# Two attention heads at a time on the two halves of TensorE's array, and value products that come out transposed

## The chip, the cores and the metric

The kernel runs on one core of one Trainium2 chip. TensorE (PE) multiplies matrices into PSUM, VectorE (DVE) and ScalarE (ACT) work element by element, GpSimd (POOL) and SyncE (SP) do little here but set up and start transfers. The metric is the device time of one execution in microseconds, the median of several runs.

## The reference

Two layers over 256 tokens of width 1024 in float32. Each layer is x += 1/2 norm(FFN), x += norm(mixer), x += 1/2 norm(FFN). The mixer of the first layer is the dilated attention that the change is about; that of the second is a retention.

```python
def banded_attention(q, k, v, bias, radius):
    ...
    s = jnp.einsum('nbqhd,nbkhd->nbhqk', qb, kw).astype(jnp.float32) * (dh ** -0.5) + bias_blk
    s = jnp.where(valid[None, :, None], s, NEG_INF)
    smax = jnp.max(s, axis=-1, keepdims=True)
    p = jnp.exp(s - smax)
    denom = jnp.sum(p, axis=-1, keepdims=True)
    o = jnp.einsum('nbhqk,nbkhd->nbqhd', (p / denom).astype(v.dtype), vw)
    lse = (smax + jnp.log(denom))[..., 0]
    ...

def dilated_attention(h, w_in, w_out, rel_bias):
    proj = (h @ w_in).reshape(B, S, N_GROUPS, 3, H_A, DH_A)
    # three groups, (window, dilation) = (128, 1), (512, 4), (2048, 16): 16 heads of 64 each
    ...
    wts = jax.nn.softmax(jnp.stack(lses, axis=0), axis=0)
    o = jnp.einsum('gbsh,gbshd->bshd', wts.astype(h.dtype), jnp.stack(outs, axis=0))
    return o.reshape(B, S, D_A) @ w_out
```

Merging the three groups by their softmax denominators is the same as one softmax over the keys of all three groups. The kernel does that.

## The kernel before, in words

Everything is one sequence of weight products with small work in between. All weights stream from DRAM in their order of use (`Stream`): a transfer of 1 MB lands in `raw`, ScalarE writes its rounded part `whi`, VectorE the rest `wlo` (lines 109 to 116), and each product is three matmuls, x_hi·w_hi, x_hi·w_lo and x_lo·w_hi (`mm3`, lines 182 to 184). A piece is a quarter of a unit of 512 columns (1024 for the output weights), 12 matmuls of 128x512; a ring holds six pieces that are split ahead of their use.

`attn` goes through two octets of heads (o = 0, 1), each with nine units: q and k of the three groups, then v of the three. The tokens are in two tiles T of 128. After a unit its PSUM sums are evicted; q and k are transposed at line 624 (`qk_store`). Work between the pieces waits in two lists: `pend` is emptied after a unit's second piece, and after each piece two entries of `bg` are taken (`unit`, `work`). After the last k, `push` puts the softmax of 16 (token tile, head) combinations into `bg`, one step for each, with head i's scores in step i, its exponential in step i + 1 and its transposes in step i + 2; so two steps run after each piece of the v units:

- `sm_scores`: q of the head is 64 rows of `qk`, on partitions 0-63 or 64-127. One product with the 256 keys of group 0 (line 644) and four small ones, 64x64, for groups 1 and 2 (line 649, written to the rows of either half of the tokens); a custom VectorE instruction adds the bias and takes the minimum (line 652).
- `sm_exp`: ScalarE's exponential with the sum into `den` (line 659).
- `sm_trans`: three transposes into a bank `ptt` (line 665) and a copy into `PT`, by ScalarE for odd i (667), by VectorE for even i (669).

`pv` multiplies, for each of eight heads, `PT` as the stationary operand with 64 columns of `V` as the moving one (lines 680, 681, and 683 for either half of the rows), so the output `ob` has tokens in rows; VectorE divides by the denominators (685, 687). `o_store` transposes the result (line 696) and splits it into `ot` (699, 700). For the first octet `pv` and `o_store` are in `bg` and run within the next unit; for the second they are hooks between the rows of the output projection `down`.

PSUM has a pool of six banks for sums (`acc`: scores, products, value products) and one of two for transposes (`trb`). The instructions of an engine are ordered by a scheduler from the order in which the program issues them, except in the first unit and at the end of `down`, where the order is written out.

## Time and profile before

| | |
|---|---|
| median of 3 runs | 1352.9 us (1352.35 to 1353.52) |
| profiled execution, from first to last instruction | 1351.3 us |
| PE busy | 1335.3 us, 99% |
| VectorE busy | 855.0 us, 63% |
| ScalarE busy | 710.9 us, 53% |
| DMA | 235.46 MB, mean 174 GB/s |
| softmax of the two octets | about 285 to 330 and 428 to 474 us |
| value products | 339 to 353, 482 to 489, 492 to 498 us |

The profiled execution has no time of its own beside its span; the median of the runs is 1.6 us above the span. In the lines of the profile, `PE` is a matmul and `PEld` a weight load; `out<-in` are the program's tiles, followed by rows*columns of the stationary operand and rows x columns of the moving one; L644 is line 644 of the kernel. A product in plain float32 has two records. The records of matmuls overlap, since they are pipelined: what a matmul costs is read from the starts of its neighbours.

### The profile page before, as it was taken

Reading aid. Unit: us, or ns where it says so; the run is one execution under the profiler, and the core shown is the slowest. Engines: PE = TensorE matmul, PEld = TensorE weight load, DVE = VectorE, ACT = ScalarE, POOL = GpSimd, SP = SyncE. Lnnn points to the kernel's source line nnn. Section 1 sums busy time; section 2 is a strip of 40 time slices with the busy share of each in tenths; the row PEclk is TensorE's granted clock in tenths of the full one; section 3 lists DMA queues with packets and bytes.
Section 4 is the critical chain, followed back from the end, with each engine's and each line's share of the span. In section 5 each row is a group of like instructions: output and inputs, shape, how many; then the busy total and the mean of one; then the engine's idle time right before and its main releaser. Section 6 shows DMA issues by size and latency. Waiting matters only on the chain.

```text
span 1351.3 us, 16684 instructions
## 1 busy us (share of the span) xinstructions
PE 1335.3 (99%) x6342; PEld 1077.1 (80%) x6342; DVE 855.0 (63%) x1501; ACT 710.9 (53%) x1103; POOL 19.2 (1%) x16
## 2 busy tenths in 40 slices
PE   8999999999999999999999999999999999999997
PEld 6878887877887787888888888877888888888886
DVE  5756556575355547866557665479888775766544
ACT  4655455565355535865454655355555544565532
POOL 1000001000000001000000000000000000000000
PEclk8999999999999999999999999999999999999999
DMA  7755557753574235655555655556555545465551
GB/s 208 240 169 186 187 200 181 210 187 109 134 209 156 95 116 170 206 187 186 186 187 177 201 185 174 186 161 194 156 162 158 178 151 192 154 204 188 187 187 63
DMA packets 129693, 235.46 MB, mean 174 GB/s; under 512 B 25020, under 2 KB 41900, under 8 KB 129613
## 3 DMA queue, kind: packets, MB, share of 16 engines
q1 hardware_dynamic: 129468, 234.14, 54.6%
q8 instruction: 50, 0.82, 0.2%
q10 hardware_dynamic: 144, 0.26, 0.1%
q14 instruction: 31, 0.25, 0.1%
HBM read 232.21 MB, written 1.12 MB: 173 GB/s over the span
## 4 chain that ended last, share of the span: by engine, by line
PE 93%; DVE 3%; DMA 2%; ACT 1%; issue 1%; SPq 0%; DVEq 0%; ACTq 0%
PE ac_f L184 11%; PE ac_f L183 11%; PE ac_f L182 11%; PE d_f L182 6%; PE d_f L184 6%; PE d_f L183 6%; PE at L182 5%; PE at L184 5%; PE at L183 5%; PE rt L183 4%; PE rt L184 4%; PE rt L182 4%; PE sc L644 1%; PE htr L340 1%; PE d_rt L182 1%; PE d_rt L184 1%
## 5 line engine op out<-in xcount | busy, mean ns | idle before, releaser
L116 DVE SCALAR_TENSOR_TENSOR wlo<-raw,gcol,whi 128x512 fp32r<-128x512 f32 x596 | 418.3, 749 | 216.6 <-ACT whi L115 215.8
L115 ACT ACTIVATE whi<-raw,gcol 128x512 fp32r<-128x512 f32 x596 | 393.3, 715 | 295.6 <-PE ac_f L184 83.8
L110 DVE TENSOR_TENSOR wlo<-raw,whi 128x1024 fp32r<-128x1024 f32 x112 | 137.2, 1225 | 147.7 <-ACT whi L109 147.7
L109 ACT ACTIVATE whi<-raw 128x1024 fp32r<-128x1024 f32 x112 | 118.7, 1060 | 178.8 <-PE d_f L184 103.9
L182 PE MATMUL d_f<-whi,hhf 128*128 128x512 f32 x352 | 140.7, 400 | 0.0
L184 PE MATMUL d_f<-whi,hlf 128*128 128x512 f32 x352 | 138.7, 394 | 0.0
L183 PE MATMUL d_f<-wlo,hhf 128*128 128x512 f32 x352 | 138.2, 393 | 0.0
L182 PE MATMUL at<-whi,xh_f 128*128 128x512 f32 x276 | 111.4, 404 | 0.0
L184 PE MATMUL at<-whi,xl_f 128*128 128x512 f32 x276 | 108.4, 393 | 0.0
L183 PE MATMUL at<-wlo,xh_f 128*128 128x512 f32 x276 | 107.6, 390 | 0.0
L183 PE MATMUL rt<-wlo,xh_f 128*128 128x512 f32 x244 | 97.3, 399 | 0.0
L182 PE MATMUL rt<-whi,xh_f 128*128 128x512 f32 x244 | 96.7, 396 | 0.0
L184 PE MATMUL rt<-whi,xl_f 128*128 128x512 f32 x244 | 96.4, 395 | 0.0
L184 PEld LDWEIGHTS d_f<-whi,hlf 128*128 128x128 f32 x352 | 66.1, 188 | 16.9
L183 PEld LDWEIGHTS d_f<-wlo,hhf 128*128 128x128 f32 x352 | 66.1, 188 | 15.5
L182 PEld LDWEIGHTS d_f<-whi,hhf 128*128 128x128 f32 x352 | 66.1, 188 | 15.1
L182 PE MATMUL ac_f<-whi,xh_in 128*128 128x512 f32 x176 | 71.2, 405 | 2.9 <-ACT whi L115 2.7
L184 PE MATMUL ac_f<-whi,xl_in 128*128 128x512 f32 x176 | 69.9, 397 | 0.0
L183 PE MATMUL ac_f<-wlo,xh_in 128*128 128x512 f32 x176 | 69.7, 396 | 0.2 <-DVE wlo L116 0.2
L182 PE MATMUL ac_f<-whi,xh_at 128*128 128x512 f32 x168 | 66.6, 397 | 0.2 <-ACT xh_at L224 0.2
L184 PE MATMUL ac_f<-whi,xl_at 128*128 128x512 f32 x168 | 65.9, 392 | 0.0
L183 PE MATMUL ac_f<-wlo,xh_at 128*128 128x512 f32 x168 | 65.4, 389 | 0.0
(294 smaller groups left out, 2223.0 us busy)
## 6 DMA issues: line engine op xcount, KB each, us to landing
raw<-in_ffn_w_down_dram SPq DMA_DIRECT2D x44, 1024.0 KB, 4.9
raw<-in_ffn_w_up_dram SPq DMA_DIRECT2D x40, 1024.0 KB, 5.1
raw<-in_ffn_w_gate_dram SPq DMA_DIRECT2D x39, 1024.0 KB, 5.1
raw<-in_attn_w_in_dram SPq DMA_DIRECT2D x36, 1024.0 KB, 5.2
raw<-in_ret_w_in_dram SPq DMA_DIRECT2D x24, 1024.0 KB, 5.3
raw<-in_ret_w_in_dram SPq DMA_DIRECT2D x16, 512.0 KB, 4.0
raw<-in_ret_w_out_dram SPq DMA_DIRECT2D x8, 1024.0 KB, 5.0
raw<-in_ffn_w_gate_dram SPq DMA_DIRECT2D x10, 512.0 KB, 4.0
```

Source lines behind the costliest of these rows:

```text
L109: nc.scalar.activation(hi, raw, AF.Copy)
L110: nc.vector.tensor_tensor(out=lo, in0=raw, in1=hi.bitcast(F32), op=ALU.subtract)
L115: nc.scalar.activation(hi[:, s], raw[:, s], AF.Copy, scale=gc)
L116: nc.vector.scalar_tensor_tensor(out=lo[:, s], in0=raw[:, s], scalar=gc, in1=hi[:, s].bitcast(F32), op0=ALU.mult, op1=ALU.subtract,)
L182: mm(out, xh, wh, start=start, stop=False)
L183: mm(out, xh, wl, start=False, stop=False)
L184: mm(out, xl, wh, start=False, stop=stop)
L340: nc.tensor.transpose(tr[:, k * P : (k + 1) * P], h[:, k * P : (k + 1) * P], self.ident)
L644: nc.tensor.matmul(sc[:, c0 : c0 + 256], qk[0][ss, 0, p, T * P : (T + 1) * P], qk[0][ss, 1, p, :], start=True, stop=True)
```

## The change

`sm_scores` takes a pair of heads, one on partitions 0-63 and one on 64-127, into two PSUM banks, and issues their products in turn. A step is a pair; there are ten steps an octet instead of eighteen, each with an empty entry behind it in `bg`, so one step runs after each piece. `sm_exp` normalises the probabilities in place, before the transposes. `pv` makes `V` the stationary operand and `PT` the moving one, so the output comes out transposed, the even head of a pair in rows 0-63 and the odd one in rows 64-127; `o_store` splits it straight from PSUM, without normalising and transposing. `pr` and `m` have six buffers instead of three, and the program's scratch for POOL's dynamic transfers is set to 4096.

```diff
-                              den=sb.tile([P, 16], F32, tag="den", bufs=2, name=f"den{o}"))
+                              den=sb.tile([P, 2, 16], F32, tag="den", bufs=2, name=f"den{o}"))
                     def push(st=st):
-                        n = 16
-                        for i in range(n + 2):
-                            def step(i=i):
...
-                            self.bg.append(step)
+                        n = 8
+                        for j in range(n + 2):
+                            def step(j=j):
+                                if j < n:
+                                    self.sm_scores(st, j)
+                                if 1 <= j <= n:
+                                    self.sm_exp(st, j - 1)
+                                if j >= 2:
+                                    self.sm_trans(st, j - 2)
+                            self.bg += [step, lambda: None]
...
-    def sm_scores(self, st, i):
+    def sm_scores(self, st, j):
+        T, p = divmod(j, 4)
         qk = st["qk"]
         c0, cx = (0, 256) if T == 0 else (128, 0)
+        halves = [slice(0, 64), slice(64, 128)]
+        sc = [self.acc(f"sc{st['o']}_{j}{s}") for s in range(2)]
+        for s, ss in enumerate(halves):
+            nc.tensor.matmul(sc[s][:, c0 : c0 + 256], qk[0][ss, 0, p, T * P : (T + 1) * P], qk[0][ss, 1, p, :], start=True, stop=True)
+        for a in range(2):
+            for rr in range(2):
+                rs = slice((2 * T + rr) * 64, (2 * T + rr) * 64 + 64)
                 g = 1 + (a ^ rr)
+                for s, ss in enumerate(halves):
+                    nc.tensor.matmul(sc[s][rr * 64 : rr * 64 + 64, cx + a * 64 : cx + a * 64 + 64], qk[g][ss, 0, p, rs], qk[g][ss, 1, p, rs], start=True, stop=True)
+        for s in range(2):
+            i = 2 * j + s
+            pr = sb.tile([P, 384], F32, tag="pr", bufs=6, name=f"pr{st['o']}_{i}")
+            m = sb.tile([P, 1], F32, tag="m", bufs=6, name=f"m{st['o']}_{i}")
+            nc.vector.tensor_tensor_reduce(
...
+    def sm_exp(self, st, j):
+        den, rd = (st["den"][:, z, 2 * j : 2 * j + 2] for z in range(2))
+        for s in range(2):
+            pr = st["pr", 2 * j + s]
+            nc.scalar.activation(pr, pr, AF.Exp, bias=st["m", 2 * j + s], scale=-1.0, accum_out=den[:, s : s + 1])
+        nc.vector.reciprocal(rd, den)
+        for s in range(2):
+            pr = st["pr", 2 * j + s]
+            nc.vector.tensor_scalar(out=pr, in0=pr, scalar1=rd[:, s : s + 1], scalar2=None, op0=ALU.mult)
+
+    def sm_trans(self, st, j):
+        for i in (2 * j, 2 * j + 1):
...
     def pv(self, st, T):
-        for h in range(8):
-            i = T * 8 + h
-            hs = slice(h * 64, h * 64 + 64)
-            mm(ob[:, hs], PT[:, i, c0 : c0 + 128], V[:, 0, hs], start=True, stop=False)
-            mm(ob[:, hs], PT[:, i, c0 + 128 : c0 + 256], V[:, 1, hs], start=False, stop=False)
+        for p in range(4):
+            o = [ob[64 * s : 64 * s + 64, p * P : (p + 1) * P] for s in range(2)]
+            heads = [(s, T * 8 + 2 * p + s, slice((2 * p + s) * 64, (2 * p + s) * 64 + 64)) for s in range(2)]
+            for kt in range(2):
+                for s, i, hs in heads:
+                    mm(o[s], V[:, kt, hs], PT[:, i, c0 + kt * P : c0 + kt * P + P], start=kt == 0, stop=False)
             for rr in range(2):
-                mm(ob[rr * 64 : rr * 64 + 64, hs], PT[:, i, cx + rr * 64 : cx + rr * 64 + 64], V[:, 2 + 2 * T + rr, hs], start=False, stop=True)
-        rd = sb.tile([P, 8], F32, tag="rd", bufs=2, name=f"rd{st['o']}{T}")
-        nc.vector.reciprocal(rd, st["den"][:, T * 8 : T * 8 + 8])
-        on = sb.tile([P, 512], F32, tag="sg", bufs=2, name=f"on{st['o']}{T}")
-        nc.vector.tensor_tensor(out=on..., in0=ob..., in1=rd.unsqueeze(2).to_broadcast([P, 8, 64]), op=ALU.mult)
-        st["on", T] = on
+                for s, i, hs in heads:
+                    mm(o[s][:, rr * 64 : rr * 64 + 64], V[:, 2 + 2 * T + rr, hs], PT[:, i, cx + rr * 64 : cx + rr * 64 + 64], start=False, stop=rr == 1)
+        st["ob", T] = ob
 
     def o_store(self, st, T, ot):
-        tr = self.trb(f"ott{st['o']}{T}")
-        on = st["on", T]
-        for p in range(4):
-            nc.tensor.transpose(tr[:, p * P : (p + 1) * P], on[:, p * P : (p + 1) * P], self.ident)
-        trv = self.reverse(tr)
+        obv = self.reverse(st["ob", T])
-        nc.scalar.activation(hi, trv, AF.Copy)
-        nc.vector.tensor_tensor(out=lo, in0=trv, in1=hi.bitcast(F32), op=ALU.subtract)
+        nc.scalar.activation(hi, obv, AF.Copy)
+        nc.vector.tensor_tensor(out=lo, in0=obv, in1=hi.bitcast(F32), op=ALU.subtract)
...
-        m1 = sb.tile([P, 512], F32, tag="pr", bufs=3, name=f"m1{h}{t}")
-        m2 = sb.tile([P, 512], F32, tag="pr", bufs=3, name=f"m2{h}{t}")
+        m1 = sb.tile([P, 512], F32, tag="pr", bufs=6, name=f"m1{h}{t}")
+        m2 = sb.tile([P, 512], F32, tag="pr", bufs=6, name=f"m2{h}{t}")
...
-    nc = bacc.Bacc("TRN2", target_bir_lowering=False, num_devices=1)
+    nc = bacc.Bacc("TRN2", target_bir_lowering=False, num_devices=1, dynamic_dma_scratch_size=4096)
```

## The prediction

> **What bounds the kernel now.** I read the page first (busy time, chain), then who waited for PE's suppliers, then the order of time inside the attention stage.

> ```profile
> span 1351.3 us, 16684 instructions
> PE 1335.3 (99%) x6342; PEld 1077.1 (80%) x6342; DVE 855.0 (63%) x1501; ACT 710.9 (53%) x1103; POOL 19.2 (1%) x16
> PE 93%; DVE 3%; DMA 2%; ACT 1%; issue 1%; SPq 0%; DVEq 0%; ACTq 0%
> ```

> PE is busy 99% of the span and is 93% of the chain that ended last. The waits of PE by releaser have this as the longest:

> ```profile
> PE ac_f L182 <- ACT whi L115: 2.7, 1, 2.7
> ```

> Nothing makes PE wait in the attention stage. So what PE no longer has to do there comes off the end, until VectorE or ScalarE cannot follow. The span of 1351.3 is 1.6 us below the median of the runs, 1352.9; I keep those 1.6 us as what lies around the span and as unchanged.

> PE in the softmax steps, two heads between two pieces of weights (order of time, PE alone; a merged row's second number is its busy length, so I read starts):

> ```profile
> 301.49 0.39 PE L184 MATMUL at<-whi,xl_f 128*128 128x512 f32 x1
> 301.81 0.70 PE L644 MATMUL sc<-qk 64*128 64x256 f32 x2
> 302.43 0.46 PE L649 MATMUL sc<-qk 64*64 64x64 f32 x8
> 302.82 0.55 PE L665 MATMUL ptt<-ident,pr 128*128 128x128 f32 x3
> 303.30 0.70 PE L644 MATMUL sc<-qk 64*128 64x256 f32 x2
> 303.92 0.45 PE L649 MATMUL sc<-qk 64*64 64x64 f32 x8
> 304.31 0.55 PE L665 MATMUL ptt<-ident,pr 128*128 128x128 f32 x3
> 304.61 0.48 PE L182 MATMUL at<-whi,xh_f 128*128 128x512 f32 x1
> 304.93 0.40 PE L183 MATMUL at<-wlo,xh_f 128*128 128x512 f32 x1
> 305.17 0.39 PE L184 MATMUL at<-whi,xl_f 128*128 128x512 f32 x1
> ```

> One projection matmul takes 0.23 us (304.93 to 305.17 and its neighbours). From 301.49 to 304.93 there are 3.44 us with two of those in them, so two heads cost 2.98: per head 0.62 for the wide score product (two records: an f32 product is two passes), 0.39 for the four small ones (eight records), 0.48 for three transposes, where the last before the projection needs only 0.30. A piece of weights is 12 projection matmuls, 2.75 us, so a piece with its two heads lasts 5.73.

> The value products (order of time, PE; the first head, one in the middle, and what follows the sixteenth):

> ```profile
> 339.35 0.33 PE L680 MATMUL o<-V,PT 128*128 128x64 f32 x2
> ...
> 340.09 0.43 PE L680 MATMUL o<-V,PT 128*128 128x64 f32 x2
> 340.37 0.39 PE L681 MATMUL o<-V,PT 128*128 128x64 f32 x2
> 340.68 0.34 PE L683 MATMUL o<-V,PT 128*64 128x64 f32 x4
> 340.95 0.43 PE L680 MATMUL o<-V,PT 128*128 128x64 f32 x2
> ...
> 352.89 0.50 PE L182 MATMUL at<-whi,xh_f 128*128 128x512 f32 x1
> ```

> A head is 0.86 (340.09 to 340.95); sixteen took 13.54 (339.35 to 352.89), and there are two octets: 27.1 in all. Weights of 128 columns feed only 64 moving columns there (0.28 and 0.31 for two records), while the 64-wide products of L683 do four records in 0.27.

> **What the trace says about parts of the array side by side.** Weight loads, order of time, in a window of 10 to 20 ns:

> ```profile
> 303.92 0.14 PEld L649 LDWEIGHTS sc<-qk 64*64 64x64 f32 x2 [0.33 <-issue]
> ...
> 340.68 0.14 PEld L683 LDWEIGHTS o<-V,PT 128*64 128x64 f32 x2
> ```

> ```profile
> L649 PEld LDWEIGHTS sc<-qk x256: 129/134/135, 286.0 to 469.7; 64*64 64x64 f32 x128
> ```

> Two loads of about 134 ns each fit into 0.14 us, so two 64-column halves of the array load and run together. L649 and L683 are the products whose outputs go to rows 0-63 and 64-127. Side by side for two *row* halves appears nowhere before: consecutive heads are separated by transposes.

> **The change part by part.**

> Scores by pairs (PE, on the path). The counts do not change: two wide and eight small products and six transposes a pair. What changes is their order: each kind now comes once for a pair, with one head on rows 0-63 and the other on rows 64-127. If the halves run together, the two wide products take one head's 0.62 plus some 0.02 of offset. The eight small ones fill four quarters of the array, each with the same four records as one half has now, so 0.39 plus two more offsets, 0.42. Six transposes: the first three with their way in cost what the last three cost now, 0.30, and three more at 0.11 each (eight transposes in a row, below, take 0.79): 0.63. Ends: 0.09 before (301.49 + 0.23 to 301.81) and 0.09 after (304.61 to 304.93, less 0.23). Together 1.87 instead of 2.98, 1.11 less, for 16 pairs (2 octets, 2 token tiles, 4 pairs) 17.8. At the ends of each octet some steps have scores or transposes alone and save less. The first octet's scores begin here (chain of work), and its value products at 339.35:

> ```profile
> 285.44 0.62 PE sc L644 x2
> ```

> These 53.9 us hold eleven pieces of 2.75, so the softmax costs PE 23.6. After: two steps of scores alone (0.62 + 0.02 + 0.42 + 0.18 of ends), six full ones of 1.87, two of transposes alone (0.66): 15.0. That is 8.5 less an octet, 17.0 in all. Bounds: if the row halves run one after the other, the wide ones take 0.62 + 2 x 0.21 = 1.04 (0.21 is a 256-column record without its ends) and the small ones about 0.62, that is 0.62 more a pair, 10 us in all: then 7. If going from one row half to the other costs the ends every time (some 0.2 for each of eight small products, and two full 0.62), a pair takes about 4.1 and the scores lose 18. I take the first, since the nearest row (L649) shows two parts of the array together.

> Value products transposed (PE, on the path). Now V is stationary with 64 columns and the probabilities move: for a pair, four products of 128 columns and four of 64, two records each, alternating between the column halves that L683 uses. One half does four records of 128 columns (about 0.11 each, half of 0.21 plus little) and four of 64 (0.06: L649's four a half in 0.39 less ends of 0.15): 0.68 a pair, both halves together. The array's shape changes twice a token tile instead of sixteen times; 0.3 for that. Four token tiles: 4 x (4 x 0.68 + 0.3) = 12.1, against 27.1: 15.0 less. Bound: halves one after the other, 1.36 a pair, 23: 4 less. I take side by side, because L683 is this very shape with half the columns.

> Transposes of the output go (PE). Sixteen, in the octet o = 0 eight in a row (order of time, PE):

> ```profile
> 355.76 1.03 PE L696 MATMUL ott<-ident,on 128*128 128x128 f32 x8
> 356.55 0.47 PE L182 MATMUL at<-whi,xh_f 128*128 128x512 f32 x1
> ```

> 0.79 + 0.09 for eight, 1.8 for sixteen. `o_store` then reads the PSUM bank of the products; in `down` four banks of sums and both `ob` make six, the size of the pool, and o_store(1) comes ahead of the tail, so no product finds the pool empty.

> Normalising moves (VectorE, ScalarE; beside PE). The groups by form, the reciprocal's line, and the engines over one softmax stretch:

> ```profile
> L116 DVE SCALAR_TENSOR_TENSOR wlo<-raw,gcol,whi 128x512 fp32r<-128x512 f32 x596 | 418.3, 749 | 216.6 <-ACT whi L115 215.8
> L652 DVE CUSTOM_DVE_ANT_1 pr<-sc,bias 128x384 f32<-128x384 f32 x32 | 17.5, 551 | 8.1 <-PE sc L649 8.1
> L669 DVE COPY PT<-ptt 128x384 f32<-128x384 f32 x16 | 8.9, 554 | 3.1 <-PE ptt L665 3.1
> L876 DVE TENSOR_SCALAR rc<-rc,nw_gn 128x512 f32<-128x512 f32 x8 | 3.8, 485 | 0.2
> L589 DVE TENSOR_SCALAR V<-at,rstd_f 128x512 f32<-128x512 f32 x4 | 2.9, 750 | 1.6 <-PE at L184 1.4
> L652 DVE DVE_READ_ACCUMULATOR2_ANT m<- 128x1 f32 x32 | 2.7, 84 | 0.0
> L659 ACT ACTIVATE pr<-pr,m 128x384 f32<-128x384 f32 x32 | 19.4, 608 | 4.3 <-DVE m L652 4.1
> L659 ACT ACTIVATION_READ_ACCUMULATOR pr<-pr,m 128x1 f32 x32 | 6.0, 188 | 0.0
> L685 DVE RECIPROCAL rd<-den x4: 202/203/204, 306.6 to 472.0; 128x8 f32<-128x8 f32 x4
> 286.00:336.00 50.00, 50.00 (x325) 35.85 (x325) 30.23 (x69) 30.26 (x65) 0.00 (x0) 1.00 0.41 123
> ```

> Added: a reciprocal (0.20) and two multiplications a pair. L876 is the same instruction from SBUF to SBUF over 512 columns, 485 ns; for 384 columns between 364 (by columns) and 485, taken as 400. That is 1.0 us of VectorE a pair, 16 us in all, where four normalisations of the output and their four reciprocals went. VectorE has 30.2 of 50 now. Per piece and pair it then holds 1.50 (two splits), 1.27 (two score reductions with their reads), 0.55 (a copy) and 1.0: 4.32; over ten pieces of an octet with eight pairs, four evictions of V at 0.75 and two copies of keys some 42, against PE's 27.5 + 15.0 = 42.5. The cover is almost used up: VectorE becomes a second bound. The splits run up to six pieces ahead of PE (the ring), so a lag of one or two microseconds is absorbed; I charge 0.5 us an octet, 1.0 in all, with bounds of 0 and 6 (the multiplication at L589's 750 gives 5.6 us more an octet, of which part shows).

> The added wait: VectorE's reciprocal waits for ScalarE's exponentials, and behind it on VectorE stand the next splits and copies; PE's transposes wait for the multiplications. From the end of a pair's scores: reduction 0.64, two exponentials 2 x 0.80, reciprocal 0.20, two multiplications 0.80: 3.2, and 6 if each engine has two splits ahead of it. The transposes come two steps later, 2 x 4.6 = 9.2 us. Nothing waits while the lag stays under 3 us.

> No cost: the `pr` and `m` buffers (six instead of three) also serve `rotary`, whose rows wait for no buffer; the list of steps grows from nine pieces' worth to ten, and eleven pieces lie between the scores and the value products (285.44 to 339.35 in the chain); POOL issues none of the transfers, so its smaller scratch has no user.

> Sum: 17.0 + 15.0 + 1.8 - 1.0 = 32.8. 1352.9 - 32.8 = 1320.1.

> [...]

> **The rivals.**
> 1. Tiles in strict order: a product's first pass starts only after the second pass of the one before. The value products alternate halves, so each second pass covers the next first one and their term stays. The wide score products take three turns of 0.21 and ends of 0.20, 0.84 instead of 0.64; the small ones eight of 0.06 and some 0.18, 0.66 instead of 0.42; 16 x 0.44 = 7 us. 1327. For it: row halves together are not shown. Against: L649 and L683.
> 2. The row halves don't run together (the change doesn't do what it says for the scores): 10 less gain, 1330; with the small ones paying the array's ends as well, up to 1355, within what is called no change.
> 3. VectorE becomes the bound in both softmax stretches: up to 6 us, 1326 instead of 1320; for it the 42 against 42.5.
> 4. Slower: PE stands at the first transpose of every pair, waiting for the multiplications, because VectorE's queue has its splits for later pieces ahead of them. It decides from 33.8 / 16 = 2.1 us a pair on, that is when the way from scores to normalised rows takes over 9.2 + 2.1 = 11.3 instead of 3 to 6; at 2.6 us a pair the time is 1361. Against: VectorE would have to lag 5 us, more than its sums give.

> **How the numbers follow.** About 0.2% (2.7 us) is what a measurement of this kernel tells from no change. Forecast (1313 to 1324) 0.54; strict order 0.13; row halves apart 0.14 (of it 0.03 near no change); VectorE bound 0.12; slower 0.05; still faster than 1313 0.02. Faster 0.92, same 0.03, slower 0.05. The range leaves out the slow rival and the ends: 1310 to 1335.

> **What would show it.** Right: in the order of time a pair's L644 records (four) lie within 0.7 us and its small ones within 0.45; the value products of a token tile take about 3 us; no `ott` rows; PE still 99%. Wrong: L644's four records spread over 1.0 us (halves apart), the small ones over 0.65 (strict order), PE waiting at `ptt` for VectorE's `pr`, VectorE over 95% in the softmax stretch.

## The result, and the profile after

The changed kernel takes 1318.7 us (median; 1317.18 to 1320.59), the kernel before 1352.6: a ratio of 0.9756, with an interval of 0.9743 to 0.9768, 33.9 us less. The forecast was 1320.1.

The page of the changed kernel, its span, busy times and chain:

```profile
span 1315.1 us, 16640 instructions
PE 1298.9 (99%) x6326; PEld 1051.8 (80%) x6326; DVE 864.7 (66%) x1541; ACT 712.1 (54%) x1103; POOL 19.4 (1%) x16
PE 90%; DVE 4%; DMA 3%; ACT 2%; issue 1%; SPq 0%; DVEq 0%; ACTq 0%
```

PE is still busy for 99%, its busy time is 36.4 us shorter, and the span is 36.2 us shorter. VectorE gained 9.7 us of work. PE's longest wait lies, as before, in the first unit and not in the attention:

```profile
PE ac_f L182 <- ACT whi L115: 1.9, 2, 1.5
```

One softmax step of a pair, PE in order of time (the scores are now lines 644 and 650, the transposes 676):

```profile
300.75 0.40 PE L184 MATMUL at<-whi,xl_f 128*128 128x512 f32 x1
301.08 0.70 PE L644 MATMUL sc<-qk 64*128 64x256 f32 x4
301.71 0.46 PE L650 MATMUL sc<-qk 64*64 64x64 f32 x16
302.10 0.87 PE L676 MATMUL ptt<-ident,pr 128*128 128x128 f32 x6
302.73 0.48 PE L182 MATMUL at<-whi,xh_f 128*128 128x512 f32 x1
303.05 0.40 PE L183 MATMUL at<-wlo,xh_f 128*128 128x512 f32 x1
```

Four records of the wide products now take what two took (0.63, starts 301.08 to 301.71), sixteen of the small ones what eight took (0.39), six transposes 0.63. From 300.75 to 303.05 there are 2.30 us with two projections of 0.23 in them: 1.84 a pair, where two heads took 2.98.

The value products (lines 693, 696), a token tile's first two pairs and the beginning of the third, and what follows the eighth pair:

```profile
329.03 0.66 PE L693 MATMUL o<-PT,V 128*64 128x128 f32 x8
329.52 0.40 PE L696 MATMUL o<-PT,V 128*64 128x64 f32 x8
329.75 0.61 PE L693 MATMUL o<-PT,V 128*64 128x128 f32 x8
330.19 0.40 PE L696 MATMUL o<-PT,V 128*64 128x64 f32 x8
330.42 0.61 PE L693 MATMUL o<-PT,V 128*64 128x128 f32 x8
...
334.54 0.51 PE L182 MATMUL at<-whi,xh_f 128*128 128x512 f32 x1
```

A pair takes 0.67 (329.75 to 330.42), both token tiles 5.51, where they took 13.54.

To place the gain, I take the attention by itself: from its first projection to the first product of the FFN behind it. The rows by tile give both starts (durations, then first and last start); the first two rows are of before, the others of after:

```profile
L182 PE MATMUL at<-whi,xh_f x276: 387/394/502, 206.3 to 478.5; 128*128 128x512 f32 x138
L182 PE MATMUL ac_f<-whi,xh_at x168: 387/394/496, 517.4 to 643.8; 128*128 128x512 f32 x168
```

```profile
L182 PE MATMUL at<-whi,xh_f x276: 387/394/505, 204.8 to 450.3; 128*128 128x512 f32 x138
L182 PE MATMUL ac_f<-whi,xh_at x168: 387/388/503, 480.7 to 607.1; 128*128 128x512 f32 x168
```

Before 517.4 - 206.3 = 311.1, after 480.7 - 204.8 = 275.9: 35.2 less. The other 1.0 of the 36.2 between the two spans is the run-up (206.3 against 204.8, less 0.5 given back behind the attention); over all runs of this study the attention's start moved between 204.7 and 207.1, and for the changed kernel, run twice, it is 204.8 and 206.9. The same difference of starts, from one profiled execution of each kernel, is the measure below that this run-up doesn't disturb. Two columns say where in the attention PE's time went: from the start of each of its records to the start of the next, added up by tile (`sc` and `ptt`; `o` and, before, `ott`). What is left, mostly projections, is 238.5 to 238.6 in every kernel but three, named below.

| kernel | attention, us | against after | scores and their transposes | value products, output transposes | median, us |
|---|---|---|---|---|---|
| before | 311.1 | +35.2 | 44.1 | 28.5 | 1352.6 |
| after | 275.9 | | 26.2 | 11.2 | 1318.7 |
| after, once more | 276.0 | +0.1 | 26.2 | 11.2 | 1319.4 |
| scores alone | 293.3 | +17.4 | 26.2 | 28.5 | 1333.6 |
| products alone | 294.3 | +18.4 | 44.2 | 11.2 | 1335.7 |
| pairs on one half | 287.0 | +11.1 | 37.3 | 11.2 | 1330.2 |
| order, pair by pair | 281.8 | +5.9 | 26.6 | 16.7 | 1324.7 |
| order, tile by tile | 285.6 | +9.7 | 26.2 | 21.0 | 1327.8 |
| blocks of four | 276.0 | +0.1 | 26.2 | 11.3 | 1317.3 |
| no normalising | 276.0 | +0.1 | 26.2 | 11.2 | 1318.0 |
| 1 multiplication more | 276.1 | +0.2 | 26.4 | 11.2 | 1318.9 |
| 2 more | 278.1 | +2.2 | 26.6 | 11.5 | 1319.5 |
| 4 more | 282.2 | +6.3 | 30.4 | 11.8 | 1324.5 |
| quarters | 272.7 | -3.2 | 23.1 | 11.2 | 1313.3 |

The three are products alone (239.0), 2 more (240.1) and 4 more (239.9).

### The profile page after: what moved, and what is told of

The parts are those of the page before. It is cut to its first block, busy times and chain, and to the rows that moved or that the text cites. A ratio compares the mean times of both kernels' runs of the same rounds, so it can differ in the third digit from the quotient of the medians.

```text
span 1315.1 us, 16640 instructions
## 1 busy us (share of the span) xinstructions
PE 1298.9 (99%) x6326; PEld 1051.8 (80%) x6326; DVE 864.7 (66%) x1541; ACT 712.1 (54%) x1103; POOL 19.4 (1%) x16
## 4 chain that ended last, share of the span: by engine, by line
PE 90%; DVE 4%; DMA 3%; ACT 2%; issue 1%; SPq 0%; DVEq 0%; ACTq 0%
PE ac_f L184 12%; PE ac_f L183 12%; PE ac_f L182 12%; PE d_f L182 6%; PE d_f L184 6%; PE d_f L183 6%; PE at L182 5%; PE at L184 5%; PE at L183 5%; PE rt L184 4%; PE rt L183 4%; PE rt L182 4%; PE htr L340 1%; DMA raw<-in_ret_w_in_dram 1%; DMA raw<-in_ffn_w_gate_dram 1%; PE ptt L676 1%
## 5 line engine op out<-in xcount | busy, mean ns | idle before, releaser
L116 DVE SCALAR_TENSOR_TENSOR wlo<-raw,gcol,whi 128x512 fp32r<-128x512 f32 x596 | 417.2, 747 | 191.2 <-ACT whi L115 190.6
L115 ACT ACTIVATE whi<-raw,gcol 128x512 fp32r<-128x512 f32 x596 | 393.8, 715 | 273.2 <-PE ac_f L184 87.1
L182 PE MATMUL d_f<-whi,hhf 128*128 128x512 f32 x352 | 140.7, 400 | 0.0
L184 PE MATMUL d_f<-whi,hlf 128*128 128x512 f32 x352 | 138.8, 394 | 0.0
L183 PE MATMUL d_f<-wlo,hhf 128*128 128x512 f32 x352 | 138.2, 393 | 0.0
L182 PE MATMUL at<-whi,xh_f 128*128 128x512 f32 x276 | 111.6, 404 | 0.0
L184 PE MATMUL at<-whi,xl_f 128*128 128x512 f32 x276 | 108.3, 392 | 0.0
L183 PE MATMUL at<-wlo,xh_f 128*128 128x512 f32 x276 | 107.4, 389 | 0.0
L183 PE MATMUL rt<-wlo,xh_f 128*128 128x512 f32 x244 | 97.1, 398 | 0.0
L182 PE MATMUL rt<-whi,xh_f 128*128 128x512 f32 x244 | 96.7, 396 | 0.0
L184 PE MATMUL rt<-whi,xl_f 128*128 128x512 f32 x244 | 96.4, 395 | 0.0
L184 PEld LDWEIGHTS d_f<-whi,hlf 128*128 128x128 f32 x352 | 66.1, 188 | 17.1
L183 PEld LDWEIGHTS d_f<-wlo,hhf 128*128 128x128 f32 x352 | 66.1, 188 | 15.4
L182 PEld LDWEIGHTS d_f<-whi,hhf 128*128 128x128 f32 x352 | 66.1, 188 | 15.1
L182 PE MATMUL ac_f<-whi,xh_in 128*128 128x512 f32 x176 | 70.4, 400 | 2.2 <-ACT whi L115 1.9
L183 PE MATMUL ac_f<-wlo,xh_in 128*128 128x512 f32 x176 | 69.1, 392 | 1.2 <-DVE wlo L116 1.2
L184 PE MATMUL ac_f<-whi,xl_in 128*128 128x512 f32 x176 | 69.3, 394 | 0.0
L184 PE MATMUL ac_f<-whi,xl_at 128*128 128x512 f32 x168 | 66.2, 394 | 0.0
L182 PE MATMUL ac_f<-whi,xh_at 128*128 128x512 f32 x168 | 65.8, 393 | 0.2 <-ACT xh_at L224 0.2
L183 PE MATMUL ac_f<-wlo,xh_at 128*128 128x512 f32 x168 | 65.9, 392 | 0.0
```

Of the source, the lines that this page charges most:

```text
L115: nc.scalar.activation(hi[:, s], raw[:, s], AF.Copy, scale=gc)
L116: nc.vector.scalar_tensor_tensor(out=lo[:, s], in0=raw[:, s], scalar=gc, in1=hi[:, s].bitcast(F32), op0=ALU.mult, op1=ALU.subtract,)
L182: mm(out, xh, wh, start=start, stop=False)
L183: mm(out, xh, wl, start=False, stop=False)
L184: mm(out, xl, wh, start=False, stop=stop)
```

## The experiments

Ratios are to the kernel before, measured beside each run.

**Each part alone.** Theory A is that of the prediction: the parts of the array run side by side, and PE's time adds up. First the scores alone, with the old value products:

```diff
-        nc.vector.reciprocal(rd, den)
-        for s in range(2):
-            ... nc.vector.tensor_scalar(out=pr, in0=pr, scalar1=rd[:, s : s + 1], ...)
+        # pv, its division and o_store as in the kernel before
```

> The changed kernel with the value products, the division by the denominators after them and the output transposes of the kernel before: the scores by pairs alone. My sum: the scores by pairs give 17.0 to 17.6 of the gain, so 1335 to 1336. If the parts of the change hide each other (a rival: something else sets the end once PE is shorter), the one part alone gives as much as both, 1319 to 1325.

Measured: 1333.55, ratio 0.986 (0.9845 to 0.9875); the attention is 17.8 us shorter than before. Then the products alone:

```diff
     def sm_exp(self, st, i):   # of the kernel before, head by head
+        self.nc.vector.reciprocal(rd, den)
+        self.nc.vector.tensor_scalar(out=pr, in0=pr, scalar1=rd, scalar2=None, op0=ALU.mult)
     # pv and o_store of the changed kernel
```

> The kernel before, with its scores head by head, but normalised before the transposes and with the value products transposed: the second part of the change alone. My sum: 15.0 for the products and 1.8 for the transposes that go, 1352.6 - 16.8 = 1336; VectorE has ample room, since PE's steps are as long as before. If the normalising on VectorE costs something of its own, less gain: 1338 to 1342.

Measured: 1335.73, ratio 0.9873 (0.9856 to 0.9889); the attention is 16.8 us shorter. The two add up to 34.6 of the 35.2. So nothing else sets the end when both are in. Most of the missing 0.6 was lost in this run, not gained together: its value products take 11.2 as in the changed kernel, but its projections and score steps take 0.5 longer than before, with no new wait of PE. Transposes stand by themselves between two projections nine times there, five times before, which is the likely reason.

**Side by side, or only fewer changes of shape?** The scores could gain merely because each shape comes once for two heads. Here the pairs are heads 0 and 2, 4 and 6, 1 and 3, 5 and 7, which lie on the same rows:

```diff
-        for s, ss in enumerate(halves):
+        for s, (p, ss) in enumerate((h // 2, halves[h % 2]) for h in pairs):   # pairs = (h, h + 2)
```

> The changed kernel, but the two heads of a pair lie on the same half of the array's rows (0 and 2, 4 and 6, 1 and 3, 5 and 7), everything else as it is, so the shapes change as seldom as in the changed kernel. Theory A (the scores gain because the two row halves run together): the wide products take 1.04 instead of 0.63 a pair and the small ones 0.62 instead of 0.39, 16 x 0.64 = 10 us more, 1329. Theory C (they gain because each shape comes once for two heads instead of once for one): no change, 1318.7.

Measured: 1330.17, ratio 0.9832 (0.9818 to 0.9847), attention 11.1 longer than after. PE in order of time:

```profile
299.18 1.13 PE L644 MATMUL sc<-qk 64*128 64x256 f32 x4
300.23 0.73 PE L650 MATMUL sc<-qk 64*64 64x64 f32 x16
300.89 0.87 PE L685 MATMUL ptt<-ident,pr 128*128 128x128 f32 x6
```

The same records take 1.05 instead of 0.63 and 0.66 instead of 0.39. So of the 17.8 us of the scores 11.1 come from running on both halves, all of them in the score products. The other 6.7 come with each kind standing once for two heads, so that the shape changes half as often: against before, this run has 4.9 less in the score products and 1.9 less in the transposes. Theory A holds, and theory C has a share.

**Must the products alternate?** Rival 1 said that products of different parts start strictly in program order. First one half's products before the other's, within a pair:

```diff
-            for kt in range(2):
-                for s, i, hs in heads:
+            for s, i, hs in heads:
+                for kt in range(2):
                     mm(o[s], V[:, kt, hs], ...)
-            for rr in range(2):
-                for s, i, hs in heads:
+                for rr in range(2):
                     mm(o[s][:, rr * 64 : rr * 64 + 64], ...)
 # and in sm_scores: for s, for rr, for a, instead of for a, for rr, for s
```

> The changed kernel, but one half's products all come before the other half's: the four small score products of the even head before those of the odd one, and the four value products (eight records) of the even head before those of the odd one. Theory A with tiles that start out of program order: no change, 1318.7. Theory B (tiles overlap, but in program order): the value products take 1.3 instead of 0.67 a pair, 16 x 0.6 = 10 us, and the small scores 0.66 instead of 0.39, 4 us: 1332.

Measured: 1324.65, ratio 0.9791 (0.9776 to 0.9806), attention 5.9 longer: neither. Of this 5.6 are in the value products and 0.3 in the scores. The scores, PE in order of time:

```profile
298.33 0.70 PE L644 MATMUL sc<-qk 64*128 64x256 f32 x4
298.97 0.48 PE L650 MATMUL sc<-qk 64*64 64x64 f32 x16
299.38 0.87 PE L676 MATMUL ptt<-ident,pr 128*128 128x128 f32 x6
```

The small scores take 0.41 instead of 0.39, although four records of each quarter now stand ahead of the next quarter's: they did start out of order. In a window from 298.965 to 299.012 the first record of each quarter has begun; one quarter's own records come 0.06 apart or more:

```profile
298.97 0.31 PE L650 MATMUL sc<-qk 64*64 64x64 f32 x4
```

The value products did not keep together. The odd head's first record (L693, 128 columns) starts when the even head has begun the fifth of its eight (L695, 64 columns), and a head takes 0.49 (331.48 to 331.97):

```profile
331.47 0.22 PE L695 MATMUL o<-PT,V 128*64 128x64 f32 x1
331.48 0.32 PE L693 MATMUL o<-PT,V 128*64 128x128 f32 x1
331.53 0.28 PE L695 MATMUL o<-PT,V 128*64 128x64 f32 x2
...
331.97 0.32 PE L693 MATMUL o<-PT,V 128*64 128x128 f32 x1
```

Then all 16 products of a tile's even heads ahead of the odd ones:

```diff
-        for p in range(4):
+        for s in range(2):
+            for p in range(4):
                 # two products with 128 columns, then two with 64, of head 2 p + s
```

> The changed kernel, but in pv all 16 products (32 records) of the even heads of a token tile come before the 16 of the odd heads. Theory A without a limit to how far ahead a product may start: no change, 1318.7. With a limit of some 16 records: part of the overlap goes, 3 to 8 us. Theory B or a limit of a few records: the halves run one after the other, 4 token tiles x 4 x 0.67 = 10.7 us more, 1329.

Measured: 1327.77, ratio 0.9813 (0.9797 to 0.9829), attention 9.7 longer. Here the even half runs alone, 0.67 for one head, until near the end of its block (PE in order of time):

```profile
332.21 0.40 PE L695 MATMUL o<-PT,V 128*64 128x64 f32 x4
332.45 0.60 PE L693 MATMUL o<-PT,V 128*64 128x128 f32 x4
332.88 0.22 PE L695 MATMUL o<-PT,V 128*64 128x64 f32 x1
332.89 0.32 PE L693 MATMUL o<-PT,V 128*64 128x128 f32 x1
332.94 0.28 PE L695 MATMUL o<-PT,V 128*64 128x64 f32 x2
333.05 0.27 PE L693 MATMUL o<-PT,V 128*64 128x128 f32 x1
333.06 0.22 PE L695 MATMUL o<-PT,V 128*64 128x64 f32 x1
```

The odd half's first record starts at 332.89, just when the even half has begun the first of its last four (332.88, two from 332.94, 333.06). In the run before, too, the odd half started with four of the even half's records to go, and in its scores four records of a quarter stood ahead of the next quarter's, and all started together. All three fit theory F: a part of the array takes about four records ahead, and only what stands behind more than these waits for its place in the program. Its test is blocks of four:

```diff
+            for s, i, hs in heads:
+                for kt in range(2):
+                    mm(o[s], V[:, kt, hs], ...)
+            for s, i, hs in heads:
+                for rr in range(2):
+                    mm(o[s][:, rr * 64 : rr * 64 + 64], ...)
```

> The changed kernel, but in pv two products (four records) of the even head come before two of the odd one, and so on. Theory F, from the two runs with other orders: a part of the array takes up to four records ahead of time, and what stands behind them waits in program order. Then blocks of four cost next to nothing: 1318.7, up to 1319.5. Theory B (strict order): the second block starts with the last record of the first, 0.67 a pair becomes 1.0 to 1.1: 1324 to 1326.

Measured: 1317.26, ratio 0.9736 (0.9723 to 0.975), attention 276.0, as after, and a pair of the value products takes 0.67 as there (329.79 to 330.46):

```profile
329.79 0.66 PE L693 MATMUL o<-PT,V 128*64 128x128 f32 x8
330.23 0.45 PE L696 MATMUL o<-PT,V 128*64 128x64 f32 x8
330.46 0.66 PE L693 MATMUL o<-PT,V 128*64 128x128 f32 x8
```

Strict order is out, an unlimited reach is out, and the reach of four foretold this one. Whether it is counted in records or in products (four records are two products here) no run tells, and no block between four and eight was run.

**Does normalising cost anything?** Without it (the probabilities stay unnormalised):

> The changed kernel without the reciprocals and the 32 multiplications (the probabilities stay unnormalised). My sum: they lie beside PE and cost 1.0 us at most, 1317.7 to 1318.7. If VectorE bounds the softmax stretches (rival 3), up to 6 us faster, 1313.

Measured: 1317.98, ratio 0.974 (0.9726 to 0.9755); attention 276.0: nothing. Then one, two and four multiplications by 1 more for each head:

```diff
             nc.vector.tensor_scalar(out=pr, in0=pr, scalar1=rd[:, s : s + 1], scalar2=None, op0=ALU.mult)
+            for _ in range(k):   # 1, 2, 4
+                nc.vector.tensor_scalar(out=pr, in0=pr, scalar1=1.0, scalar2=None, op0=ALU.mult)
```

> The changed kernel with one multiplication by 1 more for each head, 0.84 us of VectorE a pair. In a stretch of four pairs VectorE is busy 16.7 of 18.5 us now; it would need 20.0. If the buffers ahead of PE did not absorb it, PE would lose 1.5 us in four pairs, 6 us over both octets: 1325. If the six split pieces absorb a lag of 3 us an octet, as I assume: 1319 to 1321.

Measured: 1318.88, ratio 0.9747 (0.9733 to 0.9762), attention +0.2.

> The changed kernel with two multiplications by 1 more for each head, 1.7 us of VectorE a pair: VectorE needs 23.4 us where PE takes 18.5, so it is the bound, 4.9 us in four pairs, 9.8 an octet. Without anything absorbed 20 us more, 1338; with a lag of some 5 us an octet absorbed by split pieces, 1328 to 1330. If VectorE's time were no bound at all here: 1318.7.

Measured: 1319.45, ratio 0.9753 (0.9738 to 0.9767), attention +2.2 instead of the 10 or 20 I expected: a miss. The engines in a stretch of the softmax (busy time of PE, PEld, DVE, ACT), first after, then with two more, then with four more:

```profile
296.16:314.70 18.54, 18.54 (x154) 13.64 (x152) 16.66 (x44) 13.25 (x29) 0.00 (x0) 1.00 0.33 111
```

```profile
286.00:324.00 38.00, 38.00 (x287) 27.82 (x287) 37.42 (x110) 27.37 (x60) 0.00 (x0) 1.00 0.40 133
```

```profile
286.00:324.00 38.00, 36.33 (x289) 26.21 (x287) 37.42 (x113) 24.16 (x52) 0.00 (x0) 1.00 0.36 116
324.00:345.00 21.00, 21.00 (x130) 16.85 (x131) 20.51 (x53) 12.37 (x22) 0.00 (x0) 1.00 0.64 169
```

With two more VectorE is busy 37.4 of 38 us, and PE doesn't wait in this stretch; 0.7 us of new waits, at the transposes, lie in the second octet. With four more PE loses time in the stretch (36.33 of 38).

> The changed kernel with four multiplications by 1 more for each head, 2.9 us of VectorE a pair: VectorE then needs 7.2 us a pair where PE takes 4.6, 21 us too much an octet. With two more multiplications nothing was lost although VectorE was busy 98%: it fell behind by some 9 us and made that up after the softmax. If the six split pieces absorb a lag of 10 to 12 us, 18 to 22 us are lost over both octets: 1337 to 1341. If the lag is never paid: 1319.5.

Measured: 1324.51, ratio 0.9793 (0.978 to 0.9806), attention +6.3, a third of what I expected: a miss again. VectorE stays full until 345, long after the scores: the work is put off into a time in which the changed kernel leaves half of VectorE idle (10.74 of these 21 us busy). Meanwhile PE uses pieces that were split earlier: at 334 us VectorE has ended 71 splits of the attention's pieces, against 78 in the changed kernel, for as many products begun (150 and 148). At two splits a piece that is three or four pieces less ahead, of the ring's six. Of the 6.3 us, 2.8 are waits of PE that the changed kernel doesn't have. In the other 3.5, and in 1.5 of the 2.2 with two more, PE doesn't wait; in both runs it goes ten times instead of four from a projection straight to transposes, as in the products alone, so work in a worse order is likely, but no run separates it.

**A better version.** Each wide product is cut in two, so that all score products have one shape:

```diff
-        for s, ss in enumerate(halves):
-            nc.tensor.matmul(sc[s][:, c0 : c0 + 256], qk[0][ss, 0, p, T * P : (T + 1) * P], qk[0][ss, 1, p, :], ...)
+        for rr in range(2):
+            for s, ss in enumerate(halves):
+                q = slice(T * P + rr * 64, T * P + rr * 64 + 64)
+                nc.tensor.matmul(sc[s][rr * 64 : rr * 64 + 64, c0 : c0 + 256], qk[0][ss, 0, p, q], qk[0][ss, 1, p, :], ...)
```

> The changed kernel with each wide score product cut into its two 64-column halves, so that all score products are 64x64 in shape and all four quarters of the array run the wide ones together. The change of shape between wide and small products (about 0.09 of draining a pair) goes, and the exposed weight loads are half as long (0.05 less, twice): 16 x 0.19 = 3 us less, 1315.7. Rival: two quarters that read the same 256 moving columns share a way in, and the wide products take longer: up to 16 x 0.4 = 6 us more.

Measured: 1313.31, ratio 0.971 (0.9697 to 0.9723), against 1319.38 and 0.9749 (0.9735 to 0.9762) for the changed kernel on the same chip:

> The changed kernel once more, on the same chip as the three below, to compare them with: 1318.7.

The attention is 3.2 us shorter, as expected, all of it in the scores. The medians are 6.1 apart; in the two profiled executions, 6.8 apart, 3.5 lie outside the attention, where the kernels are the same, so I count the 3.2 alone. (Blocks of four, with the attention of the changed kernel, has a median 2.1 lower too.) PE in order of time:

```profile
300.13 0.66 PE L646 MATMUL sc<-qk 64*64 64x256 f32 x8
300.61 0.41 PE L652 MATMUL sc<-qk 64*64 64x64 f32 x16
300.96 0.87 PE L678 MATMUL ptt<-ident,pr 128*128 128x128 f32 x6
```

Wide and small products take 0.83 a pair instead of 1.02: the wide 0.48 instead of 0.63, the small 0.34 instead of 0.39. A wide product's weight load takes 131 ns instead of 184 (medians), the 0.05 less that was put down, but not half. Four quarters that read the same columns two by two don't hold each other up: two wide records in each of them take 0.48 (300.13 to 300.61), no more than two in each half did in the changed kernel (0.63), where two more in turn, with pairs on one half, added 0.42 (1.05).

## Why the prediction was right

*What bounds it.* PE was busy for 99% and its time came off the end: 36.4 us less busy, 36.2 us less span.

*Scores.* 17.0 predicted, 17.8 measured alone. The pair was put at 1.87 and took 1.84; the small products of four quarters take 0.39 rather than 0.42. The choice of side by side over one after the other was worth about the 10 us that the bound said: 11.1 measured, 0.69 a pair (the bound wrote 0.62, and its terms add up to 0.60).

*Value products and transposes.* 15.0 and 1.8 predicted, 16.8 measured alone. That these agree to the tenth is luck: by PE's own starts the value products went from 27.0 to 11.2, 15.8 less, the output transposes took 1.5 and not 1.8, and the run with the products alone lost 0.5 elsewhere. The pair was put at 0.68 and took 0.67; the 0.3 that was put down for the changes of shape in each token tile was too much (2.76 a tile, 5.51 / 2, instead of 3.02).

*Normalising.* 1.0 us was charged and nothing was lost: with it and without it the attention takes 276 us. Here the working was off, not only careful. VectorE was put at 42 of 42.5 us an octet, 99%; it is busy 16.66 of 18.54, 90%. I had added up mean durations, but VectorE's instructions overlap: in this stretch their durations add up to 19.45. A reduction and its read were put at 0.635; in the order of time of the changed kernel the next one starts 0.48 later:

```profile
303.33 0.55 DVE L655 CUSTOM_DVE_ANT_1 pr<-sc,bias 128x384 f32<-128x384 f32 x1
...
303.81 0.08 DVE L655 DVE_READ_ACCUMULATOR2_ANT m<- 128x1 f32 x1
303.81 0.55 DVE L655 CUSTOM_DVE_ANT_1 pr<-sc,bias 128x384 f32<-128x384 f32 x1
...
304.28 0.08 DVE L655 DVE_READ_ACCUMULATOR2_ANT m<- 128x1 f32 x1
```

The multiplication was put at 400 ns and takes 415 (mean of one, by form):

```profile
L669 DVE TENSOR_SCALAR pr<-pr,den 128x384 f32<-128x384 f32 x16 | 6.0, 415 | 0.2
```

And a VectorE that is full would have cost little at once: 2.2 us at 98%.

*The sum.* 32.8 was predicted; the attention lost 35.2 and the median 33.9. Of the 2.4 in the attention 1.0 is the lag that didn't come, 0.9 the scores and their transposes (17.9 by PE's starts), 0.8 the value products, less 0.3 for the output transposes. The median has the run-up of several executions in it, and fell by less.

*The rivals.* Strict order (1327): out, in a form that I had not thought of, since the order does count beyond four records (blocks of eight cost 5.6 us in the value products, blocks of four nothing); in the order as the change has it, nothing is lost. In the run with one half's products first, four quarters' first records start within 0.04 us of each other with others of the program between them, and with all even heads first an odd product's record (332.89) starts ahead of even ones (332.94). The trace of the kernel before already spoke against it: the first records of the two L683 products start at 340.68 and 340.69, ahead of the second records at 340.79 and 340.80, if a product's two records stand in a row in the program. Row halves apart (1330): out, and built on purpose it gives 1330.2. VectorE as the bound (1326): out at this load. PE waiting for the multiplications (1361): no such wait in PE's list for the attention.

## What to carry to other kernels

When a product uses half of the array's rows or columns, pair it with one on the other half and issue them in turn, or in blocks of at most four records to a half (276.0 us of attention against 275.9 here; blocks of eight cost 5.6); here 11.1 of the 17.8 us of the scores came from that and 6.7 from changing shape half as often. Then bring neighbouring products to one shape, even at the price of more instructions: cutting the wide ones in two gave another 3.2 us. Work that is moved to another engine needs room over the whole stretch until its buffers run out, not in each step: here VectorE at 98% cost 2.2 us, of which 0.7 were waits.
